# One streaming encoder layer on one core: root-scaled turning matmuls in the opening, and a last feed-forward group run by token halves

## The chip, the cores and the metric

The kernel runs on one core of one Trainium2 chip. The metric is device time in microseconds (us) for one launch, median over runs. Engines are named as in the profile: PE is TensorE (PEld its weight load), DVE is VectorE, ACT is ScalarE, POOL is GpSimd, SP is SyncE, which here issues DMAs. A bank is one of the eight 2-KB-per-partition buffers in which PE leaves its results.

## The reference, cut to what matters

One layer over 512 prompt tokens and 64 sample tokens (576 together), model width 1024, all in fp32:

```
n = rmsnorm(x, ln_mix);  proj = n @ w_in
h = x + W_out [ GDN(conv, gates of proj) ; DiffAttn(proj) ]
h = h + MemCrossAttn(rmsnorm(h, ln_mem_q))
h = h + W2 relu(W1 rmsnorm(h, ln_ffn))^2        (1024 -> 4096 -> 1024)
y = rmsnorm(h, ln_final)
rmsnorm(x, g) = x * rsqrt(mean(x*x) + 1e-6) * g
```

Outputs are y for both groups of tokens, and new caches and states. The change touches the first norm (and the turning of its result) and the last group of the feed-forward part with the final norm.

## The kernel before, in words

**Layout.** Activations are kept with features on partitions and tokens along the free axis, as `[128, 4, 576]` tiles, two for 1024 features. x arrives with tokens on partitions, as five token tiles (four of 128, one of 64; `TT`), and must be turned. Every projection is split for precision: an operand is held as `hi`, its value rounded to fp32r, and `lo`, the rest, and `project` (L150) adds hi x hi, hi x lo and lo x hi, so 24 matmuls for 1024 features into one bank. It does so for each of two token halves (`HALVES`: columns 0 to 256 and 256 to 576). `weights` (L141) loads 128 columns of a weight matrix into one of three `raw` tiles (tag `raw`, `bufs=3`), casts `hi` on ACT (L147) and subtracts `lo` on DVE (L148) into two buffers each (tags `wh`, `wl`).

**Who sets the order.** A scheduler orders each engine's queue by program order and readiness. The opening is written out by hand: inside `with in_order()` (L281) each engine's instructions keep the order of the program, though instructions from elsewhere may come between them.

**Opening (L204 to L331).** SP's queue loads, in this order, token tile 0, the row of `ln_mix` spread over 128 partitions (`gain_rows`, L117), tile 1, weights 4 of `w_in`, tiles 2 and 3, weights 5, tile 4, weights 6, and then the rows of all gains, of the convolution weights and of its state, into one tile `rows` of 126 partitions. For each token tile ACT squares and sums (`squares`, L190), DVE and POOL make the root (`root`, L195; `rpow` on POOL, L174), DVE scales the whole 128 x 1024 tile by root and gain (`scale`, L201), PE turns it in eight 128 x 128 transposes into two banks (`turn`, L204), ACT copies `hi` (L244) and DVE subtracts `lo` (L249). Between them PE runs the first token half of three projections (`first_half`, weights 4, 5, 6), as soon as tiles 0 and 1 are turned. The splits of weights 5 and 6 are on POOL (L304, L315). Last come the transpose of `rows` into the columns `gcol` and the third first half.

**Beside the opening.** PE also turns the unscaled x (8 x 5 transposes into banks `g0` and `g1`, L367) for the residual stream. It stands later in the program, but nothing holds it back: the scheduler puts these transposes wherever PE is free.

**End (L955 to L1000).** The feed-forward part is done in eight groups of 512 hidden features: `ff1(g)` makes four blocks of hidden features, `ff2(g)` adds their product to the residual `hT`, eight blocks of 128 output features, each for both token halves. ff1 of a group is issued ahead of ff2 of the group before. In the last group `add_residual(m, True)` also squares on ACT (L866, L869) and sums on DVE (L871). After it ACT multiplies each block by `ln_final` (L987), five matmuls against ones sum over the features for each token tile (`norm_columns`, L875), DVE and POOL make the roots, and for each token tile and half PE turns four blocks back into a bank of tag `ba` (which has two banks), ACT (half 0, L996) or DVE (half 1, L998) multiplies by the root, and SP stores the tile (L1000).

Banks by tag: `pr` 3, `ba` 2, `g0`, `g1` and `gs` one each.

## Time and profile before

| | us |
|---|---|
| runs shown, median of 3 | 1105.75 (1105.25 to 1108.7) |
| the profiled execution | 1104.43 |
| its span in the profile | 1102.7 |
| PE busy / idle in the span | 1056.7 / 46.0 |
| DVE, ACT, POOL busy | 623.8, 408.4, 78.6 |

In a row of the profile, `L98 PE MATMUL pr<-u,wh 128*128 128x256 f32 x16` is line 98, its engine and operation, the tile written and those read, the stationary and the moving shape, and the count. A row in order of time begins with its start and its length in us and ends with the idle time of the engine before it and what ended it. A row of groups has total busy time, mean in ns, and idle time before. An fp32 matmul appears as two instructions, an fp32r one and a transpose as one. A matmul's length contains the latency of the pipeline; the pace is read from a run of them.

### The profile page before, as it was taken

The page shows a single profiled execution, that of the slowest core. Times are in us where ns is not written, and L with a number is a line of the kernel's source. Part 1 is how long each engine was busy: PE and PEld are TensorE (multiplying, and loading weights), DVE is VectorE, ACT ScalarE, POOL GpSimd, SP SyncE. Part 2 cuts the span into 40 slices and gives each one's busy share as a digit, 9 for nine tenths or more (in the row PEclk, how much of TensorE's full clock was granted, in tenths as well). Part 3 has the DMA queues.
Part 4 walks back from the last instruction along what each step waited for, and adds up shares of the span by engine and source line. Part 5 has one row for each costly group of instructions (what it writes and reads, how often), then busy time and mean ns, then how long its engine had stood idle before and what let it go on. Part 6 is the DMA issues. An engine that isn't in the chain of part 4 may idle for free.

```text
span 1102.7 us, 18954 instructions
## 1 busy us (share of the span) xinstructions
PE 1056.7 (96%) x7708; PEld 1002.8 (91%) x7708; DVE 623.8 (57%) x1335; ACT 408.4 (37%) x842; POOL 78.6 (7%) x127
## 2 busy tenths in 40 slices
PE   5999899899999999899999999999999999999997
PEld 5999799888888888799988799999999999999996
DVE  6766674665455566355454555655555555455554
ACT  5533554233135557543332343322222222222244
POOL 5421120221000000000000000000000000000000
PEclk9999999999999999899999999999999999999998
DMA  7242310100122254434211032223323141414122
GB/s 220 84 141 71 117 39 21 41 20 12 48 78 60 91 171 118 134 117 151 69 47 39 23 93 78 59 72 92 86 77 96 58 116 49 115 50 114 58 78 86
DMA packets 151494, 90.62 MB, mean 82 GB/s; under 512 B 5472, under 2 KB 147934, under 8 KB 150896
## 3 DMA queue, kind: packets, MB, share of 16 engines
q1 hardware_dynamic: 151408, 89.41, 27.6%
q8 instruction: 61, 1.00, 0.4%
q14 instruction: 25, 0.20, 0.1%
HBM read 79.66 MB, written 9.74 MB: 81 GB/s over the span
## 4 chain that ended last, share of the span: by engine, by line
issue 41%; PE 30%; DVE 1%; DMA 1%; ACT 1%; POOL 1%; POOLq 0%; ACTq 0%; SPq 0%
PE pr L98 20%; PE g L98 4%; PE ba L102 3%; PE gs L98 2%; PE ba L98 2%; DMA out_dram<-p 1%; POOL ta L174 0%; DVE an L805 0%; POOL tiny L174 0%; PE g L102 0%; DVE u L998 0%; ACT p L840 0%; DVE wl L148 0%; POOLq L1031 0%; ACT p L927 0%
## 5 line engine op out<-in xcount | busy, mean ns | idle before, releaser
L98 PE MATMUL pr<-u,wh 128*128 128x256 f32 (+1 forms) x3936 | 811.5, 300 | 0.4
L98 PEld LDWEIGHTS pr<-u,wh 128*128 128x128 f32 x3936 | 638.2, 191 | 7.0 <-issue 2.0
L98 PE MATMUL pr<-u,wl 128*128 128x256 f32 (+1 forms) x1968 | 584.9, 298 | 0.0
L98 PEld LDWEIGHTS pr<-u,wl 128*128 128x128 f32 x1968 | 373.2, 190 | 1.3 <-issue 0.2
L147 ACT CAST wh<-raw 128x1024 fp32r<-128x1024 f32 (+1 forms) x161 | 141.4, 878 | 289.0 <-PE pr L98 266.2
L148 DVE TENSOR_TENSOR wl<-raw,wh 128x1024 fp32r<-128x1024 f32 (+1 forms) x161 | 163.0, 1012 | 66.5 <-ACT wh L147 62.2
L858 DVE TENSOR_TENSOR u<-u,pr 128x256 f32<-128x256 f32 (+1 forms) x160 | 72.4, 453 | 105.2 <-PE pr L98 105.2
L964 DVE TENSOR_TENSOR p<-pr,rB 128x256 f32<-128x256 f32 x64 | 29.3, 458 | 65.4 <-PE pr L98 65.4
L167 ACT CAST u<-p 128x256 fp32r<-128x256 f32 x64 | 27.8, 434 | 89.2 <-DVE p L965 87.5
L174 POOL TENSOR_TENSOR tiny<-tiny,nhalf 128x1 f32<-128x1 f32 (+2 forms) x10 | 10.3, 1032 | 658.7 <-DVE tiny L882 488.3
L168 DVE TENSOR_TENSOR u<-p,u 128x256 fp32r<-128x256 f32 x64 | 29.2, 457 | 20.2 <-ACT u L167 20.2
L98 PE MATMUL g<-u,qz 128*128 128x256 f32 (+4 forms) x96 | 29.2, 405 | 1.2 <-ACT p L781 1.2
L965 DVE SCALAR_TENSOR_TENSOR p<-p 128x256 f32<-128x256 f32 x64 | 29.3, 458 | 1.7
L102 PE MATMUL ba<-ident,u 128*128 128x128 f32 (+2 forms) x128 | 22.7, 318 | 6.0 <-ACT p L840 3.2
L355 DVE SCALAR_TENSOR_TENSOR p<-p,gcol,p 128x579 f32<-128x579 f32 x33 | 27.1, 820 | 0.9
L98 PE MATMUL g<-Dt,B 128*128 128x128 f32 (+1 forms) x200 | 26.6, 278 | 0.9 <-DVE B L571 0.9
L571 DVE SCALAR_TENSOR_TENSOR B<-lev,At 128x512 f32<-128x512 f32 (+1 forms) x30 | 20.9, 708 | 10.0 <-PE g L98 6.9
L98 PEld LDWEIGHTS g<-Dt,B 128*128 128x128 f32 (+1 forms) x200 | 22.7, 185 | 4.0 <-ACT X L602 2.9
L781 ACT ACTIVATE p<-g,ta 128x320 f32<-128x320 f32 (+4 forms) x40 | 21.2, 532 | 13.6 <-DVE ta L779 10.4
L98 PE MATMUL g<-Y,X 128*128 128x128 f32 (+1 forms) x192 | 25.6, 274 | 0.2
L602 ACT COPY X<-g 128x512 f32<-128x512 f32 (+1 forms) x24 | 13.2, 549 | 33.7 <-PE g L102 33.6
L170 ACT ACTIVATE u<-u,gcol 128x256 fp32r<-128x256 f32 (+1 forms) x32 | 17.1, 533 | 23.1 <-DVE u L858 23.1
(270 smaller groups left out, 981.6 us busy)
## 6 DMA issues: line engine op xcount, KB each, us to landing
raw<-in_w_ff_dram SPq DMA_DIRECT2D x32, 512.0 KB
raw<-in_w_ff_dram SPq DMA_DIRECT2D x64, 256.0 KB
raw<-in_w_in_dram SPq DMA_DIRECT2D x28, 512.0 KB
raw<-in_w_mem_k_dram SPq DMA_DIRECT2D x8, 512.0 KB
raw<-in_w_mem_v_dram SPq DMA_DIRECT2D x8, 512.0 KB
raw<-in_w_out_dram SPq DMA_DIRECT2D x8, 512.0 KB
raw<-in_w_mem_q_dram SPq DMA_DIRECT2D x8, 512.0 KB
raw<-in_w_mem_o_dram SPq DMA_DIRECT2D x8, 512.0 KB
```

The source lines that it names most:

```text
L98: nc.tensor.matmul(out, lhsT, rhs, start=start, stop=stop)
L102: nc.tensor.transpose(out, in_, ident[:n, :n])
L147: A.copy(wh, raw)
L148: V.tensor_tensor(wl, raw, wh.bitcast(F32), ALU.subtract)
L167: A.copy(h, src)
L168: V.tensor_tensor(lo, src, h.bitcast(F32), ALU.subtract)
L355: V.scalar_tensor_tensor(yv[:, :n], cb[:, i : i + n], cwt[:, m, i : i + 1], yv[:, :n], ALU.mult, ALU.add)
L571: V.scalar_tensor_tensor(B[:n, :, :n], lev[:n, :n].unsqueeze(1).to_broadcast([n, 4, n]), float(lv), At[:n, :, :n], ALU.is_equal, ALU.mult,)
L781: A.activation(p[:, :nk], b[:, :nk], AF.Exp, bias=mx[:, c : c + 1], scale=0.125, accum_out=l[:, c : c + 1])
L858: V.tensor_tensor(hm, hm, b, ALU.add)
L964: V.tensor_tensor(f, b, rB[:, a0 : a0 + n], ALU.mult)
L965: V.scalar_tensor_tensor(f, f, 0.0, f, ALU.max, ALU.mult)
```

## The change

Opening:

- The rows of the gains (42 partitions) are loaded first of all, on ACT's DMA queue, into a tile of their own; the rows of convolution weights and state stay last on SP's queue. The broadcast load of `ln_mix` is gone. PE turns the 42 rows into the columns `gmix` at once.
- x is not scaled. For each token tile DVE writes the roots on a diagonal (`root_diag`), and PE turns and scales in one matmul: stationary the 128 x 128 block of raw x, moving the diagonal (`turn_normed`). One bank now holds one block of 128 features for a whole token half.
- `hi_lo`: ACT makes `hi` with the gain as a column scale, DVE `lo` with a scalar_tensor_tensor. The first token half takes banks `pr` and `ba` in turn, the second `g0` and `ba`.
- The splits of weights 5 and 6 move from POOL to DVE.
- The order is: both first roots, split of weights 4, first half turned (root 2 after its fourth block), first halves with weights 4 and 5 with roots 3 and 4 in between, second half turned, convolution rows turned, first half with weights 6.
- The transposes of raw x and their copies are queued behind the last instruction of the opening on PE and on ACT. What followed POOL's last instruction of the opening follows DVE's last one instead, and so does the small lambda block.

End:

- While the second-last group's products run, the last group's weights are loaded, cast and split, all eight blocks, into tiles that ff1's input no longer needs.
- The last group runs its eight blocks for token half 0 and then for token half 1. The final gain is applied in the evacuation.
- Within the second pass PE also runs the root matmuls of token tiles 0 and 1 (after block 1), their turnings (after blocks 3 and 4) and the first-half turnings of tiles 2 to 4 (after block 6, into `g0`, `g1`, `gs`). Their first instructions are pinned to that place in PE's queue. After it come the roots of tiles 2 to 4 and the rest. Each token tile is stored in two halves.

The diff, cut to its core:

```diff
@@ -94,12 +95,16 @@
...
-    def mm(out, lhsT, rhs, start=True, stop=True):
-        nc.tensor.matmul(out, lhsT, rhs, start=start, stop=stop)
-    def tr(out, in_):
+    def mm(out, lhsT, rhs, start=True, stop=True, pin=False):
+        i = nc.tensor.matmul(out, lhsT, rhs, start=start, stop=stop)
+        if pin:
+            tc.keep_in_program_order(i)
+    def tr(out, in_, pin=False):
...
-        nc.tensor.transpose(out, in_, ident[:n, :n])
+        i = nc.tensor.transpose(out, in_, ident[:n, :n])
+        if pin:
+            tc.keep_in_program_order(i)
...
@@ -212,43 +216,50 @@
...
+    rows, crow = small("B0", [42, P]), small("B1", [84, P])
+    for i, g in enumerate((ln_mix[0], ln_mem_kv[0], ln_mem_q[0], ln_ffn[0], ln_final)):
+        nc.scalar.dma_start(rows[8 * i : 8 * i + 8, :], g.rearrange("(k p) -> k p", p=P))
+    nc.scalar.dma_start(rows[40:41, :], gdn_norm)
+    nc.scalar.dma_start(rows[41:42, :], diff_norm)
+    FIRST = (4, 5, 6)
+    raws = {}
...
-    gmix = gain_rows(ln_mix[0], "qz0")
...
-    FIRST = (4, 5, 6)
-    raws = {4: load(w2, 4 * P)}
+    raws[4] = load(w2, 4 * P)
...
-    rows = small("B0", [126, P])
-    for i, g in enumerate((ln_mix[0], ln_mem_kv[0], ln_mem_q[0], ln_ffn[0], ln_final)):
-        nc.sync.dma_start(rows[8 * i : 8 * i + 8, :], g.rearrange("(k p) -> k p", p=P))
-    nc.sync.dma_start(rows[40:41, :], gdn_norm)
-    nc.sync.dma_start(rows[41:42, :], diff_norm)
...
-        nc.sync.dma_start(rows[42 + 12 * i : 54 + 12 * i, :], conv_w[0, i].rearrange("(m p) -> m p", p=P))
+        nc.sync.dma_start(crow[12 * i : 12 * i + 12, :], conv_w[0, i].rearrange("(m p) -> m p", p=P))
...
-        nc.sync.dma_start(rows[90 + 12 * i : 102 + 12 * i, :], state_gdn_conv[0, 0, i].rearrange("(m p) -> m p", p=P))
-    tags = ("pr", "ba")
-    turned = {}
-    def turn_tile(t):
-        turned[t] = [turn(xn[t], TT[t][1], q, tags[q]) for q in range(2)]
-    def hi(t):
-        t0, n = TT[t]
-        for q in range(2):
-            A.copy(xh[q][:, :, t0 : t0 + n], turned[t][q])
-    def lo(t):
-        t0, n = TT[t]
-        for q in range(2):
-            V.tensor_tensor(
-                xl[q][:, :, t0 : t0 + n], turned[t][q], xh[q][:, :, t0 : t0 + n].bitcast(F32), ALU.subtract
-            )
+        nc.sync.dma_start(crow[48 + 12 * i : 60 + 12 * i, :], state_gdn_conv[0, 0, i].rearrange("(m p) -> m p", p=P))
+    diag = [small("aT", [P, 4, P]), small("aT", [P, 4, P])]
+    dg = [diag[t // 4][:, t % 4, :] for t in range(5)]
+    def turn_normed(k, half, tag):
+        a0, n = HALVES[half]
+        b = bank(tag)
+        for t in ((0, 1), (2, 3, 4))[half]:
+            t0, w = TT[t]
+            mm(b[:, t0 - a0 : t0 - a0 + w], xt[t][:w, k * P : (k + 1) * P], dg[t][:w, :w])
+        return b[:, :n]
+    def hi_lo(b, k, half):
+        a0, n = HALVES[half]
+        g = gmix[:, k : k + 1]
+        h, lo = (x[k // 4][:, k % 4, a0 : a0 + n] for x in xs)
+        A.activation(h, b, AF.Identity, scale=g)
+        V.scalar_tensor_tensor(lo, b, g, h.bitcast(F32), ALU.mult, ALU.subtract)
+    def root_diag(t, n):
+        s1 = tiny([P, 1])
+        A.activation(sqd[:n, :D], xt[t][:n], AF.Square, accum_out=s1[:n])
+        r1 = root(s1, n)
+        V.tensor_scalar(dg[t][:n, :n], ident[:n, :n], r1[:n], None, ALU.mult)
...
@@ -277,63 +288,47 @@
...
-    sqr, rts = {}, {}
-    with in_order():
-        sqr[0] = squares(xn[0], xt[0], P)
-        rts[0] = root(sqr[0], P)
-        scale(xn[0], xt[0], rts[0], gmix, P)
+    gps0 = bank("gs")
+    gmix = const([P, 42], "gmix")
+    with in_order() as opened:
+        tr(gps0[:, :42], rows)
+        V.tensor_copy(gmix, gps0[:, :42])
+        root_diag(0, P)
+        root_diag(1, P)
...
-        sqr[1] = squares(xn[1], xt[1], P)
-        rts[1] = root(sqr[1], P)
...
-        turn_tile(0)
-        hi(0)
-        sqr[2] = squares(xn[2], xt[2], P)
-        scale(xn[1], xt[1], rts[1], gmix, P)
-        turn_tile(1)
-        lo(0)
-        rts[2] = root(sqr[2], P)
-        hi(1)
-        lo(1)
+        for k in range(KT):
+            hi_lo(turn_normed(k, 0, ("pr", "ba")[k % 2]), k, 0)
+            if k == 3:
+                root_diag(2, P)
...
-        sqr[3] = squares(xn[3], xt[3], P)
-        rts[3] = root(sqr[3], P)
-        scale(xn[2], xt[2], rts[2], gmix, P)
-        turn_tile(2)
...
-        G.tensor_tensor(wts[5][1], raws[5], wts[5][0].bitcast(F32), ALU.subtract)
-        sqr[4] = squares(xn[4], xt[4], DEC)
-        rts[4] = root(sqr[4], DEC)
+        V.tensor_tensor(wts[5][1], raws[5], wts[5][0].bitcast(F32), ALU.subtract)
+        root_diag(3, P)
+        root_diag(4, DEC)
...
-        scale(xn[3], xt[3], rts[3], gmix, P)
-        scale(xn[4], xt[4], rts[4], gmix, DEC)
...
-        hi(2)
-        lo(2)
...
-        last_pool = G.tensor_tensor(wts[6][1], raws[6], wts[6][0].bitcast(F32), ALU.subtract)
-        turn_tile(3)
-        turn_tile(4)
-        hi(3)
-        lo(3)
-        hi(4)
-        lo(4)
+        V.tensor_tensor(wts[6][1], raws[6], wts[6][0].bitcast(F32), ALU.subtract)
+        for k in range(KT):
+            hi_lo(turn_normed(k, 1, ("g0", "ba")[k % 2]), k, 1)
...
-        tr(gps[:, :126], rows)
-        gcol = const([P, 126], "gcol")
-        V.tensor_copy(gcol, gps[:, :126])
+        tr(gps[:, :84], crow)
+        gcol = const([P, 84], "gcol")
+        last_dve = V.tensor_copy(gcol, gps[:, :84])
...
+    last_pool = zeroed[6]
...
-    gn = gcol[:, 40:41]
+    gn = gmix[:, 40:41]
...
-    V.tensor_scalar(dn, gcol[:, 41:42], 1.0 - LAM0, None, ALU.mult)
-    cwt = gcol[:, 42:].rearrange("p (s m) -> p m s", m=12)
+    V.tensor_scalar(dn, gmix[:, 41:42], 1.0 - LAM0, None, ALU.mult)
+    cwt = gcol.rearrange("p (s m) -> p m s", m=12)
...
@@ -363,8 +358,9 @@
...
-                for q in range(2):
-                    A.copy(hst[q][:, :, t0 : t0 + n], turn(xt[t], n, q, f"g{q}"))
+                with tc.issue_after(opened[mybir.EngineType.Activation]), tc.issue_after(opened[mybir.EngineType.PE]):
+                    for q in range(2):
+                        A.copy(hst[q][:, :, t0 : t0 + n], turn(xt[t], n, q, f"g{q}"))
...
@@ -463,7 +459,7 @@
...
-    with tc.issue_after(last_pool.ins):
+    with tc.issue_after(last_dve.ins):
...
@@ -968,36 +965,89 @@
...
-    def ff2(g, s):
-        for m in range(KT):
-            project(
-                weights(w_ff2[0, g * 512 : (g + 1) * 512, :], m * P, 4), s, add_residual(m, g == NG - 1), kt=4
-            )
+    wlast = []
+    def last_weights(m):
+        if m == 0:
+            wlast.extend(unit(i, [P, 4, 4, P], F32R) for i in (8, 7, 6, 4))
+        hi, lo = wlast[m // 4][:, m % 4], wlast[2 + m // 4][:, m % 4]
+        raw = wp.tile([P, 4, P], F32, tag="raw", name=nm("raw"), bufs=3)
+        nc.sync.dma_start(raw, w_ff2[0, (NG - 1) * 512 :, m * P : (m + 1) * P].rearrange("(k p) n -> p k n", p=P))
+        A.copy(hi, raw)
+        V.tensor_tensor(lo, raw, hi.bitcast(F32), ALU.subtract)
+    def last_block(m, s, a0, n):
+        hi, lo = wlast[m // 4][:, m % 4], wlast[2 + m // 4][:, m % 4]
+        def evac(b, a0, n):
+            add_residual(m, True)(b, a0, n)
+            hm = hT[m // 4][:, m % 4, a0 : a0 + n]
+            A.activation(hm, hm, AF.Identity, scale=gmix[:, G_FIN + m : G_FIN + m + 1])
+        project((hi, lo), s, evac, kt=4, halves=((a0, n),))
+    yo = {}
+    def turn_out(t, half, tag, pin=False):
+        t0, n = TT[t]
+        b = bank(tag)
+        for i in range(4):
+            tr(b[:n, i * P : (i + 1) * P], hT[half][:, i, t0 : t0 + n], pin=pin and i == 0)
+        return b
+    def put_out(t, half, b, r):
+        t0, n = TT[t]
+        if half == 0:
+            yo[t] = unit((10, 11, 2, 3, 5)[t], [P, 2, 512])
+            A.activation(yo[t][:n, half, :], b[:n], AF.Identity, scale=r[:n, t : t + 1])
+        else:
+            V.tensor_scalar(yo[t][:n, half, :], b[:n], r[:n, t : t + 1], None, ALU.mult)
+        dst = y_prompt[0, t0 : t0 + n] if t < 4 else y_sample[0]
+        nc.sync.dma_start(dst[:, 512 * half : 512 * half + 512], yo[t][:n, half, :])
+    def final_roots(ts, pin=False):
+        b = bank()
+        c = slice(ts[0], ts[-1] + 1)
+        r, r2 = tiny([P, 8]), tiny([P, 8])
+        V.memset(r, 1.0)
+        for t in ts:
+            t0, n = TT[t]
+            mm(b[:n, t : t + 1], accs[0][:, t0 : t0 + n], ones[:, 0:1], pin=pin and t == ts[0])
+            V.tensor_scalar(r[:n, t : t + 1], b[:n, t : t + 1], 1.0 / D, EPS, ALU.mult, ALU.add)
+        rpow(r2[:, c], r[:, c])
+        return r2
...
-        ff2(g - 1, pend)
+        for m in range(KT):
+            project(
+                weights(w_ff2[0, (g - 1) * 512 : g * 512, :], m * P, 4), pend, add_residual(m, False), kt=4
+            )
+            if g == NG - 1:
+                last_weights(m)
...
-    ff2(NG - 1, pend)
...
-        hm = hT[m // 4][:, m % 4, :]
-        A.activation(hm, hm, AF.Identity, scale=gcol[:, G_FIN + m : G_FIN + m + 1])
-    r = norm_columns()
-    for t, (t0, n) in enumerate(TT):
-        yo = unit((10, 11, 2, 3, 5)[t], [P, 2, 512])
-        for half in range(2):
-            b = bank()
-            for i in range(4):
-                tr(b[:n, i * P : (i + 1) * P], hT[half][:, i, t0 : t0 + n])
-            if half == 0:
-                A.activation(yo[:n, half, :], b[:n], AF.Identity, scale=r[:n, t : t + 1])
-            else:
-                V.tensor_scalar(yo[:n, half, :], b[:n], r[:n, t : t + 1], None, ALU.mult)
-        dst = y_prompt[0, t0 : t0 + n, :] if t < 4 else y_sample[0]
-        nc.sync.dma_start(dst, yo[:n].rearrange("p a b -> p (a b)"))
+        last_block(m, pend, *HALVES[0])
+    early = {}
+    for m in range(KT):
+        last_block(m, pend, *HALVES[1])
+        if m == 1:
+            r = final_roots((0, 1), pin=True)
+        if m in (3, 4):
+            t = m - 3
+            for half in range(2):
+                put_out(t, half, turn_out(t, half, "ba", pin=True), r)
+        if m == 6:
+            for t in (2, 3, 4):
+                early[t] = turn_out(t, 0, ("g0", "g1", "gs")[t - 2], pin=True)
+    r = final_roots((2, 3, 4))
+    for t in (2, 3, 4):
+        put_out(t, 0, early[t], r)
+        put_out(t, 1, turn_out(t, 1, "pr"), r)
...
```

Likewise left out are `lpr`, `le` and the lambda loads, which move unchanged under `tc.issue_after(last_dve.ins)`, the names `gcol` that become `gmix`, and `in_order`, which now yields the last instruction of each engine.

33 lines of the change are left out of this document (17 added, 16 removed).

## Prediction

> **What bounds the kernel now.** I read the page first (busy shares, slices, chain), then the busy time by stage (each row: the stretch, its length, busy time of PE, weight load, DVE, ACT and POOL with instructions, granted clock, DMA share, GB/s), then both ends of the kernel in order of time.
>
> ```profile
> span 1102.7 us, 18954 instructions
> PE 1056.7 (96%) x7708; PEld 1002.8 (91%) x7708; DVE 623.8 (57%) x1335; ACT 408.4 (37%) x842; POOL 78.6 (7%) x127
> PE   5999899899999999899999999999999999999997
> issue 41%; PE 30%; DVE 1%; DMA 1%; ACT 1%; POOL 1%; POOLq 0%; ACTq 0%; SPq 0%
> ...
> 0.00:10.00 10.00, 3.62 (x16) 3.25 (x17) 1.89 (x4) 4.86 (x9) 1.84 (x11) 1.00 0.84 264
> 10.00:20.00 10.00, 7.57 (x51) 7.33 (x49) 8.41 (x13) 7.32 (x14) 5.38 (x4) 0.83 0.73 186
> 20.00:30.00 10.00, 7.64 (x58) 7.20 (x56) 9.14 (x13) 4.92 (x10) 9.80 (x18) 0.89 0.68 168
> 60.00:70.00 10.00, 10.00 (x77) 10.00 (x76) 7.73 (x12) 2.79 (x6) 2.16 (x6) 1.00 0.54 148
> 1080.00:1090.00 10.00, 8.05 (x61) 7.51 (x60) 4.99 (x13) 4.79 (x9) 1.17 (x1) 0.96 0.01 2
> 1090.00:1103.00 13.00, 6.94 (x32) 5.15 (x32) 3.48 (x5) 3.17 (x5) 0.00 (x0) 0.63 0.49 182
> ```
>
> TensorE (PE) is busy for 96% and carries the chain ("issue" there is time in which it waited for nothing). The change touches its two thin ends: the first 30 us, where PE idles 6.38 + 2.43 + 2.36 = 11.2 us, and the last 23 us, where it idles 1.95 + 6.06 = 8.0 us. At 60 us it never idles, and by the slices hardly anywhere between, so work pushed from an end into the middle costs its full length.
>
> **The opening.** Rows in order of time, one of the stages, one of the chain, and the groups by shape:
>
> ```profile
> 4.46 1.06 ACT L192 ACTIVATE u<-u 128x1024 f32<-128x1024 f32 x1 [2.15 <-DMA u<-in_x_prompt_dram]
> 5.95 0.56 POOL L174 TENSOR_TENSOR tiny<-tiny,nhalf 128x1 f32<-128x1 f32 x1 [4.28 <-DVE tiny L197]
> 7.73 1.06 ACT L192 ACTIVATE u<-u 128x1024 f32<-128x1024 f32 x1 [2.12 <-DMA u<-in_x_prompt_dram]
> 9.64 0.69 DVE L285 CAST wh<-raw 128x1024 fp32r<-128x1024 f32 x1 [1.80 <-DMA raw<-in_w_in_dram]
> 10.36 1.23 DVE L288 TENSOR_TENSOR wl<-raw,wh 128x1024 fp32r<-128x1024 f32 x1
> 10.48 1.54 POOL L174 TENSOR_TENSOR tiny<-tiny,nhalf 128x1 f32<-128x1 f32 x1 [3.72 <-DVE tiny L197]
> 15.28 3.13 PE L98 MATMUL pr<-u,wh 128*128 128x256 f32 x16
> 19.20 0.60 PE L102 MATMUL pr<-ident,u 128*128 128x128 f32 x4
> 19.99 2.16 PE L98 MATMUL pr<-u,wh 128*128 128x256 f32 x16
> 22.13 3.42 DVE L202 SCALAR_TENSOR_TENSOR u<-u,tiny,gB 64x1024 f32<-64x1024 f32 x1 [0.44 <-POOL p L271]
> 27.74 4.60 PE L98 MATMUL pr<-u,u 128*128 128x256 f32 x24
> ...
> 27.70:30.00 2.30, 2.30 (x13) 2.30 (x12) 1.88 (x8) 1.23 (x3) 2.10 (x7) 0.50 0.33 33
> ...
> 273.59 0.60 PE g L98 x8
> ...
> L102 PE MATMUL g<-ident,u 128*128 128x128 f32 x20 | 4.6, 385 | 4.6 <-DMA u<-in_x_prompt_dram 4.6
> L170 ACT ACTIVATE u<-u,gcol 128x320 fp32r<-128x320 f32 x16 | 8.9, 559 | 0.0
> L170 ACT ACTIVATE u<-u,gcol 128x256 fp32r<-128x256 f32 x16 | 8.1, 508 | 23.1 <-DVE u L858 23.1
> L171 DVE SCALAR_TENSOR_TENSOR u<-u,gcol,u 128x320 fp32r<-128x320 f32 x16 | 8.7, 545 | 0.0
> L171 DVE SCALAR_TENSOR_TENSOR u<-u,gcol,u 128x256 fp32r<-128x256 f32 x16 | 7.7, 483 | 8.1 <-ACT u L170 8.1
> ```
>
> The mark is the end of the third first-half block (weights 6): 27.74 + 4.60 = 32.34 us, after which PE is full. A block is 24 matmuls: 0.12 us each at full clock (the row at 19.99, less the latency of its last), 0.2 at half clock (15.28: 3.13 us for 16; the granted clock of the 27.70 row is 0.50).
>
> The change, queue by queue:
> - **Second token tile.** The 512-KB broadcast of the gain between tiles 0 and 1 goes. The two took 7.73 - 4.46 = 3.27 us, so tile 1 lands near 4.46 + 1.63 = 6.1 (bounds 6.1 and 7.73), and weights 4 by about 8.0. The seven row loads move from SP's queue to ACT's, ahead of its first squares; ACT has little else until 4.46, so I cost them at nothing (if that cover fails, +1). DVE's queue now begins with the copy of these rows, and everything on DVE waits if they land after 7.
> - **Roots.** POOL starts 0.43 after the squares end (5.95 against 5.52) and takes 0.56, since DVE stands still for it (1.54, beside the 1.23-us DVE operation, is the other bound); the diagonal is an eighth of the 0.69-us cast's width, say 0.25 (bounds 0.1 and 0.69). 6.1 + 1.06 + 0.43 + 0.56 + 0.25: both diagonals stand at 8.4. The full-width scalings, the 3.42 at 22.13 among them, vanish.
> - **First turning.** DVE casts and splits weights 4 (0.69 + 1.23) up to 10.4 and then subtracts eight times 0.48. Between the fourth and fifth it stands for tile 2's root: ACT has done four 0.51-us copies by 11.2, then 1.06 + 0.43 + 0.56 + 0.25 make 13.5. Last subtraction at 15.5. PE turns for the same price as before: an fp32 128x128 matmul is two instructions, four of them take 0.60 us (273.59), as do four transposes (19.20). The first block ends at 16.6 at full clock, 17.7 at half.
> - **Second block:** 24 x 0.12 = 2.9, so 19.5, or up to 21.4. DVE's splits of weights 5 and 6, taken over from POOL (1.23 each), and the roots 3 and 4 lie under it.
> - **Second turning.** Every other one goes to g0, which has one bank: matmuls 0.4, ACT 0.56, DVE 0.55, handovers 0.25 make 1.76 us for two, so eight take some 6.2: 25.7 to 27.6. Queued behind them on PE are the transpose of the convolution rows and block three.
> - **Third block,** 2.9 or 4.6: it ends between 28.6 and 32.2. I take 30.0, a mix of clocks, since PE works about half of the second turning. That is 2.3 us earlier.
> - **The moved transposes.** The 20 of the x20 row lie in the opening's gaps. They are now queued behind the opening, where PE never idles: 20 x 0.15 = **3.0 us later** there. Their ACT copies hide (ACT works 2.79 of 10 us at 60).
>
> Opening: +3.0 - 2.3 = **+0.7 us**, bounds -0.7 (28.6) and +2.9 (32.2).
>
> The Trainium skill, "TensorE: Matmul & The Clock Gate", section Terms, says that transpose mode is 4 times faster for fp32, which speaks against plain matmuls here. By it the sum would be larger by 40 x 3 x 0.15 = 18 us of PE time, an estimate; the rows at 273.59 and 19.20 disagree, and the measurement decides.
>
> **The end.** Rows in order of time, the stores by tile, and stages:
>
> ```profile
> 1085.47 0.31 PE L98 MATMUL pr<-u,wl 128*128 128x320 f32 x1
> 1087.38 0.81 PE L98 MATMUL ba<-ones,p 128*128 128x1 f32 x6 [0.77 <-DVE p L871]
> 1089.73 0.69 ACT L996 ACTIVATE u<-ba,tiny 128x512 f32<-128x512 f32 x1 [2.12 <-POOL tiny L174]
> 1097.79 0.74 DVE L998 TENSOR_SCALAR u<-ba,tiny 64x512 f32<-64x512 f32 x1 [0.72 <-PE ba L102]
> L1000 SPq DMA_DIRECT2D out_dram<-u x5: 332/356/472, 1090.6 to 1098.6; - x5
> ...
> 1098.00:1099.00 1.00, 0.00 (x0) 0.00 (x0) 0.54 (x1) 0.00 (x0) 0.00 (x0) 1.00 0.99 406
> 1100.00:1101.00 1.00, 0.00 (x0) 0.00 (x0) 0.00 (x0) 0.00 (x0) 0.00 (x0) 0.50 0.90 193
> 1101.00:1102.00 1.00, 0.00 (x0) 0.00 (x0) 0.00 (x0) 0.00 (x0) 0.00 (x0) 0.50 0.01 0
> ...
> 1060.07 0.62 ACT L147 CAST wh<-raw 128x512 fp32r<-128x512 f32 x1 [2.58 <-PE pr L98]
> 1060.72 0.69 DVE L148 TENSOR_TENSOR wl<-raw,wh 128x512 fp32r<-128x512 f32 x1
> 1063.00:1063.50 0.50, 0.50 (x6) 0.50 (x5) 0.08 (x1) 0.19 (x1) 0.00 (x0) 1.00 1.01 302
> 1063.50:1064.00 0.50, 0.50 (x6) 0.50 (x6) 0.44 (x2) 0.49 (x2) 0.00 (x0) 1.00 0.01 3
> ```
>
> The last product ends at 1085.78; the roots are out 3.95 us later (1089.73), ten evacuations end at 1098.53, data stops moving just before 1101, and the span ends about 2 us after that.
>
> The products of the last group stay the same in number. PE gains, ahead of the last one, 28 transposes (0.15 each: 4.2) and four root matmuls (6 in 0.81: 0.55): last product at 1085.78 + 4.75 = 1090.5. The first half's norm is complete more than a block before PE reaches its matmuls, and each output turning has its bank back a block later. The root chain stays 3.95: 1094.5. Then three ACT evacuations (0.69) run beside three on DVE (0.74): done at 1096.8, 1.7 us sooner. Now the stores are late: 1.25 MB fall due in 2 us instead of 8. The first is issued (0.36) at 1095.2 and moves an estimated 0.9 later; 1 MB at the 406 GB/s seen takes 2.6 us, the 64-row tile's 256 KB at 193 GB/s 1.35, so data ends at 1100.0 and the span 2 us behind, at 1102.0: -0.7. One wait is new. The roots are columns of one bank, and now DVE reads each column before the program's next root matmul writes its neighbour (before, all five matmuls came first). If PE must wait for that read, with all the products queued behind it, it costs two handovers and a short DVE operation, about 0.4: once in the second pass, twice at the end, 1.2 in all. No row shows it; between 0 and 1.2 I take 0.9, since both touch one tile. End: **+0.2 us**, bounds -2.5 (no such wait, transposes hidden in part, all stores at 406 GB/s) and +1.5 (a stall at a pinned turning besides).
>
> Moved into group 6: eight more weight loads, casts (0.62) and splits (0.69). ACT then casts for 1.24 and DVE splits for 1.38 of each block of 3.2 us (12 matmuls of 0.12, 12 of 320 columns at 0.15); they hide as long as the three raw tiles suffice.
>
> **Sum.** +0.7 + 0.2 = +0.9 us on the profiled execution's 1104.43 (span 1102.7 and 1.7 around it), 1105.3. The median of the runs shown is 1105.75; I predict **1106.6**.
>
> **The rivals.**
> - *Slower: the raw tiles run out.* In group 6 two loads per block pass through three tiles; each holds one for the issue, the landing, the cast and the split (1.31), and every other one waits for a weight buffer besides. Walked through block by block, PE stalls nowhere up to a landing 3.0 us after the issue, and 3.7 us in all at 4. For: nothing else here loads at this rate. Against: the load freed by the split's end at 1061.41 had stopped moving by 1063.5, so it lands after some 2.1 to 3. At 4 us: 1106.6 + 3.7 = 1110.3.
> - *Slower: half clock all through the opening.* Third block at 32.2: +2.9 + 0.2, 1108.9, just within 0.3%.
> - *Slower: turning matmuls at four times the 0.15.* 9.6 and 14 us of PE in turnings that last 7 and 6.2: +10, 1116.6. Against: the row at 273.59 is the same form.
> - *Faster: the moved transposes find idle PE after all,* -2.3 + 0.2: 1103.7; or both ends reach their good bounds, -0.7 - 2.5: 1102.5; both together, 1099.5. Against: they are early in the program, and the middle is full.
> - *A little faster: full clock from the first block,* since turnings are now plain matmuls: 28.6, so -0.7 + 0.2, 1105.2. The slow row at 15.28 came right after transposes. The Trainium skill's same page, section "Part 4: PE-mode transpose", says that transposes do not count as activity for the clock; the row agrees.
>
> **How the numbers follow.** A measurement of this kernel can tell about 0.3%, 3.3 us. Forecast, both ends near even: 0.36; full clock 0.10; half clock 0.10; raw tiles, or another stall that the newly ordered queues make in the middle, 0.20; dear matmuls 0.03; idle transposes or good bounds 0.21, of which 0.18 passes 3.3 us. Faster 0.18; slower 0.23 and 0.04 of the half clock, 0.27; the rest, 0.55, same. Range 1101.5 to 1111: it takes in the rivals but the dear matmuls, longer landings and the two good cases together.
>
> **What would show it.** Right: turnings start near 8.4, the third block ends near 30, all 40 raw transposes lie behind it, the span ends 11 to 12 us after the last product instead of 16.9. Wrong: PE idle in group 6 with a DMA behind it; turnings at over 0.2 us a matmul; rows landing after 7; PE waits in the middle that are not there now.

## The result and the profile after

After takes **1112.09 us** (median of 4 runs, 1111.75 to 1112.48), before in the same comparison 1105.5 (1104.23 to 1108.7): a ratio of 1.0055, 95% interval [1.0034, 1.0077]. The forecast was 1106.6 in 1101.5 to 1111, so the change is slower by 6.6 us and the time lies above the range. The profiled execution of after took 1111.75 us, its span 1110.0. Unless a ratio to another kernel is named, every ratio below is to before in the same comparison. One run of all was slow, 1162.09 us at a granted clock of 0.85, and it is the only one of its kernel (the second of experiment 6) with a trace.

The page of after (span, busy shares), then the busy time by stage in the columns that the prediction explains:

```profile
span 1110.0 us, 19049 instructions
PE 1061.5 (96%) x7749; PEld 1006.9 (91%) x7749; DVE 620.9 (56%) x1348; ACT 411.1 (37%) x854; POOL 68.2 (6%) x126
...
10.00:20.00 10.00, 9.80 (x59) 9.16 (x60) 7.16 (x15) 7.12 (x14) 1.29 (x3) 1.00 0.81 188
20.00:30.00 10.00, 9.40 (x65) 7.94 (x63) 4.83 (x10) 4.89 (x11) 2.70 (x8) 1.00 0.56 130
50.00:60.00 10.00, 7.80 (x52) 7.50 (x50) 7.33 (x10) 6.08 (x13) 1.82 (x7) 0.83 0.19 54
```

From 10 to 30 us PE is busier than before, and the clock column reads 1.00 where before had 0.83 and 0.89. That looks like the gain that was wanted, but the busy time is dearer work, and up to 15 us the pace is that of half clock all the same (rows at 14.03 and 15.39 below). And there is a new hole at 50 to 60 us: PE works 7.80 of 10 us there and the clock falls to 0.83; before, PE was full from 30 to 110 us.

To see where the time goes, I follow marks that both kernels have. The last copy of a convolution state (the last of the POOL group below, on L358 before and L353 after) stands at the end of the convolution stage. The group's columns are minimum, median and maximum duration in ns, then the first and the last start in us.

```profile
L358 POOL COPY cst<-p x11: 185/971/1272, 37.1 to 104.4; 128x3 f32<-128x3 f32 x11
```

```profile
L353 POOL COPY cst<-p x11: 187/979/981, 40.1 to 112.9; 128x3 f32<-128x3 f32 x11
```

| mark | before | after | later by |
|---|---|---|---|
| third first-half block ends | 32.34 | 34.55 | 2.2 |
| last convolution-state copy | 104.4 | 112.9 | 8.5 |
| last evacuation of the first feed-forward product starts | 1034.6 | 1044.1 | 9.5 |
| last product ends | 1085.78 | 1098.69 | 12.9 |
| span ends | 1102.7 | 1110.0 | 7.3 |

So the first 113 us lose 8.5, the middle 1.0, and the end wins 2.2. The loss of 8.5 falls into parts that can be seen. First the opening, in order of time:

```profile
8.01 0.30 PE L105 MATMUL gs<-ident,B 42*128 42x42 f32 x1 [8.01 <-DMA B<-in_diff_norm_dram]
8.35 0.20 DVE L295 COPY gmix<-gs 128x42 f32<-128x42 f32 x1 [7.41 <-PE gs L105]
10.54 0.29 DVE L262 TENSOR_SCALAR aT<-ident,tiny 128x128 f32<-128x128 f32 x1 [0.71 <-POOL tiny L178]
14.03 1.06 PE L99 MATMUL pr<-aT,u 128*128 128x128 f32 x4
15.39 0.61 PE L99 MATMUL pr<-aT,u 128*128 128x128 f32 x4
15.84 0.61 PE L99 MATMUL ba<-aT,u 128*128 128x128 f32 x4
22.61 0.97 PE L99 MATMUL g<-aT,u 128*128 128x128 f32 x6
24.79 1.07 PE L99 MATMUL g<-aT,u 128*128 128x128 f32 x6 [0.20 <-DVE u L256]
27.07 1.07 PE L99 MATMUL g<-aT,u 128*128 128x128 f32 x6 [0.20 <-DVE u L256]
31.44 3.11 PE L99 MATMUL pr<-u,u 128*128 128x256 f32 x24
```

The gain rows land at 8.0, the copy at the head of DVE's queue runs at 8.35, and the second diagonal at 10.54 to 10.83 instead of 8.4. In the first turning a block of two matmuls took 0.86 us up to the one that starts at 14.89 (14.89 - 14.03), and 15.84 - 15.39 = 0.45 after it: half pace and full pace, though the clock column reads 1.00 for both. In the second turning a pair of blocks takes 27.07 - 24.79 = 2.28 us where 1.76 was forecast.

Then the hole. These are PE, ACT and two stages of after:

```profile
51.35 1.03 PE L105 MATMUL g<-ident,u 128*128 128x128 f32 x8
55.65 1.72 PE L105 MATMUL g<-ident,u 128*128 128x128 f32 x8 [2.19 <-ACT u L363]
...
53.12 0.63 ACT L351 ACTIVATE u<-p 128x512 f32<-128x512 f32 x1 [2.22 <-DVE p L350]
53.66 1.03 ACT L151 CAST wh<-raw 128x1024 fp32r<-128x1024 f32 x1
55.01 1.07 ACT L363 COPY u<-g 128x512 f32<-128x512 f32 x2
...
55.65:58.00 2.35, 2.35 (x12) 2.33 (x13) 2.17 (x5) 1.60 (x3) 0.54 (x2) 0.57 0.33 81
58.00:60.00 2.00, 2.00 (x14) 1.93 (x12) 1.25 (x2) 1.05 (x2) 0.23 (x2) 0.66 0.55 167
```

The transposes of the unscaled x (PE L105) have one buffer of each of two banks. The first eight run at 51.35. The next eight need the banks back, and the copies that free them (ACT L363) stand in ACT's queue behind a Silu (L351), which waits 2.22 us for DVE's convolution, and behind a weight cast. PE waits 2.19 us with all the products queued behind the transposes. Right after it the granted clock is at a half: (1 - 0.57) x 2 x 2.35 + (1 - 0.66) x 2 x 2.00 = 3.4 us of half clock. Before's profile has no PE wait at all between 30 and 60 us.

At the end of after:

```profile
1095.46 1.03 PE L105 MATMUL g<-ident,u 128*128 128x128 f32 x8
1096.33 0.60 PE L105 MATMUL gs<-ident,u 128*64 128x128 f32 x4
1096.69 2.00 PE L99 MATMUL pr<-u,u 128*128 128x320 f32 x12
1103.06 1.27 ACT L1003 ACTIVATE u<-g,tiny 128x512 f32<-128x512 f32 x2 [2.75 <-POOL tiny L178]
```

Eight transposes between two products take 1096.33 - 1095.46 = 0.87 us, 0.11 each. From the last feed-forward evacuation to the last product's end it is 54.6 us instead of 51.2 (+3.4), and from there to the span's end 11.3 instead of 16.9 (-5.6).

### The profile page after: what moved, and what is told of

The parts are those of the page before. It is cut to its first block, busy times and chain, and to the rows that moved or that the text cites. A ratio compares the mean times of both kernels' runs of the same rounds, so it can differ in the third digit from the quotient of the medians.

```text
span 1110.0 us, 19049 instructions
## 1 busy us (share of the span) xinstructions
PE 1061.5 (96%) x7749; PEld 1006.9 (91%) x7749; DVE 620.9 (56%) x1348; ACT 411.1 (37%) x854; POOL 68.2 (6%) x126
## 4 chain that ended last, share of the span: by engine, by line
PE 58%; issue 2%; DVE 1%; ACT 0%; POOL 0%; DMA 0%; POOLq 0%; DVEq 0%; ACTq 0%
PE pr L99 52%; PE ba L99 2%; PE g L99 2%; PE ba L105 2%; PE gs L99 0%; DMA out_dram<-p 0%; POOL tiny L178 0%; DVE p L926 0%; DVE an L802 0%; POOL ta L178 0%; DVE u L1005 0%; ACT p L924 0%; ACT p L837 0%; ACT u L808 0%; POOLq L1081 0%
## 5 line engine op out<-in xcount | busy, mean ns | idle before, releaser
L99 PE MATMUL pr<-u,wh 128*128 128x320 f32 (+1 forms) x3808 | 787.3, 300 | 0.4
L99 PEld LDWEIGHTS pr<-u,wh 128*128 128x128 f32 x3808 | 617.8, 191 | 7.4 <-issue 2.0
L99 PE MATMUL pr<-u,wl 128*128 128x320 f32 (+1 forms) x1904 | 566.5, 299 | 0.0
L99 PEld LDWEIGHTS pr<-u,wl 128*128 128x128 f32 x1904 | 361.5, 190 | 1.3 <-issue 0.2
L151 ACT CAST wh<-raw 128x1024 fp32r<-128x1024 f32 (+1 forms) x153 | 136.9, 895 | 274.2 <-PE pr L99 253.8
L152 DVE TENSOR_TENSOR wl<-raw,wh 128x1024 fp32r<-128x1024 f32 (+1 forms) x153 | 157.5, 1030 | 70.3 <-ACT wh L151 67.1
L178 POOL TENSOR_TENSOR tiny<-tiny,nhalf 128x1 f32<-128x1 f32 (+4 forms) x11 | 8.0, 725 | 664.0 <-DVE tiny L1013 551.2
L99 PE MATMUL pr<-u,u 128*128 128x256 f32 (+1 forms) x240 | 33.7, 298 | 0.0
L99 PEld LDWEIGHTS pr<-u,u 128*128 128x128 f32 x240 | 32.2, 190 | 0.0
L778 ACT ACTIVATE p<-g,ta 128x320 f32<-128x320 f32 (+4 forms) x40 | 21.2, 533 | 12.8 <-DVE ta L776 10.4
L174 ACT ACTIVATE u<-u,gmix 128x256 fp32r<-128x256 f32 (+1 forms) x32 | 17.1, 534 | 23.2 <-DVE u L855 23.2
```

Source lines behind the costliest of these rows:

```text
L99: i = nc.tensor.matmul(out, lhsT, rhs, start=start, stop=stop)
L151: A.copy(wh, raw)
L152: V.tensor_tensor(wl, raw, wh.bitcast(F32), ALU.subtract)
L778: A.activation(p[:, :nk], b[:, :nk], AF.Exp, bias=mx[:, c : c + 1], scale=0.125, accum_out=l[:, c : c + 1])
```

## Experiments

**Theory A:** the loss is made in the opening and by the held-back transposes; the end wins 2.2. Rivals: the end loses too (B); the opening's own lateness is all of it (C); the copies' wait only moves (D).

**1. The end alone, and the opening alone.** The first kernel is before with the new end (the last hunk of the diff, with `gcol` for `gmix`), the second is after with the old end.

> The opening of before with the new end (last feed-forward group by halves, roots and output of the first half under the second). Theory A (the loss is made in the opening and the first 60 us, the end gains): no loss up to the last product, +3.4 us of added PE work there, 5.6 us less from the last product to the span's end, so 2.2 us less than before, about 1103.3. Rival B (the end loses as well, because the new stage's transposes and roots on TensorE cost more than the shorter tail gives): 1105.5 to 1108.

Measured: 1103.9 us, 0.998 [0.997, 0.9989]. A holds for the end.

The trace of this kernel shows one thing more. PE's instructions come in the same order as in before up to the last group, but in this execution the third block ended at 26.16 + 3.11 = 29.27, 3.1 us earlier than in before's profile. Two rows of it, then one of before:

```profile
51.55 0.66 PE L104 MATMUL g<-ident,u 128*128 128x128 f32 x4 [2.32 <-ACT u L371]
50.92 0.86 ACT L371 COPY u<-g 128x512 f32<-128x512 f32 x2
```

```profile
50.99 0.86 ACT L367 COPY u<-g 128x512 f32<-128x512 f32 x2
```

The copies of the unscaled x run at the same time in both, so PE, being early, waits 2.32 us for them, and the last convolution-state copy comes at 104.2 against 104.4. The wait for these copies is therefore not the new opening's alone, and an earlier third block is not worth its full length as long as they stand where they do in ACT's queue.

> The new opening with the end of before. Theory A: the whole loss and the end's missing gain, 8.5 to 9.5 us over before, 1114 to 1115. Rival B (the opening's lateness is made good in the middle, and the end loses): 1106 to 1110.

Measured: 1112.41 us, 1.0063 [1.005, 1.0075]. The opening makes the whole loss, though less than A said, and between the bounds of the two theories. Against before's 1105.66 in this comparison the two parts are +6.8 and -1.8, which add up to 5.0 us and not to the 6.6 of both; the intervals are wide enough for that. The old end was 1 us shorter here (67.1 us from the last feed-forward evacuation's start to the span's end, against 68.1 in before), since its half-clock stretch was over sooner.

**2. The held-back transposes, freed or put first.**

```diff
-                with tc.issue_after(opened[mybir.EngineType.Activation]), tc.issue_after(opened[mybir.EngineType.PE]):
-                    for q in range(2):
-                        A.copy(hst[q][:, :, t0 : t0 + n], turn(xt[t], n, q, f"g{q}"))
+                for q in range(2):
+                    A.copy(hst[q][:, :, t0 : t0 + n], turn(xt[t], n, q, f"g{q}"))
```

> After, with the forty turnings of the unscaled x for the residual no longer held behind the opening on TensorE and ScalarE: the planner may put them where it likes, as before. Theory A (3.0 us of moved transposes, 2.2 us of a wait for ScalarE's copy and about 1 us of half clock behind it all come from holding them back): 4 to 6 us less than after, about 1107. Rival C (the opening's own steps are late, and turnings among them delay the subtractions further): 1111 to 1114.

Measured: 1107.99 us, 1.0019 [1.0009, 1.0029]. The scheduler (the planner of the expectations) put 20 of the 40 transposes back into the opening's gaps; the third block still ended at 34.6, so they cost nothing there. In the second kernel they stay behind the opening, with `tc.high_priority()` added to the two holds.

> After, with the forty turnings of the unscaled x still behind the opening, but ahead of the convolution's work in ScalarE's queue, between the first projection's matmuls. Theory A (the wait of 2.2 us and the half clock come from ScalarE's copies queued behind Silu, which waits for VectorE): these 3 us go and the 3.0 us of moved transposes stay, about 1109. Rival D (the wait only moves, since ScalarE has sixteen copies of 0.5 us to do there and the first convolution then starts later): 1112 to 1114.

Measured: 1107.96 us, 1.002 [1.001, 1.0029], a little better than A's 1109. The convolution-state copies of the two kernels:

```profile
L353 POOL COPY cst<-p x11: 185/968/974, 40.2 to 109.1; 128x3 f32<-128x3 f32 x11
...
PE g L105 <- ACT u L362: 2.1, 1, 2.1
```

```profile
L353 POOL COPY cst<-p x11: 190/974/1002, 44.5 to 109.2; 128x3 f32<-128x3 f32 x11
```

The first kept the wait of 2.1 us (the row is a wait: engine and tile, releaser, us in total, times, longest) but not the half clock behind it; the second lost both. Each has the stage's end 3.7 to 3.8 us earlier than after. D and C fall. How much the place behind the opening costs can be read here too: from the end of the third block to the last state copy it is 109.2 - 34.55 = 74.6 us in the second kernel, which has neither the wait nor the half clock, and 104.4 - 32.34 = 72.1 in before, so 2.6 us.

**3. The gain copy behind the diagonals.**

```diff
-        V.tensor_copy(gmix, gps0[:, :42])
         root_diag(0, P)
         root_diag(1, P)
+        V.tensor_copy(gmix, gps0[:, :42])
```

> After, with the copy of the turned gain rows placed behind both diagonals in VectorE's written order, so that the diagonals no longer stand behind the rows' landing. Theory A (the rows land late and the copy at the head of the queue holds the diagonals back to 10.8 us): diagonals at about 8.5, first turning, its projection and everything behind 2.0 to 2.3 us earlier (third first-half block ends at 32.3 instead of 34.6), about 1110. Rival (the loads of tiles 2 to 4 or the cold clock set the pace anyway): third block at 34 to 34.6, 1112.

Measured: 1111.74 us, 1.0045 [1.0031, 1.0059], and the third block ended at 34.72. Theory A fails here: the copy was not all that held the second diagonal. In order of time, POOL and DVE of this kernel:

```profile
7.33 0.71 POOL L470 TENSOR_SCALAR_AFFINE_SELECT X<-X 128x128 f32<-128x128 f32 x1
9.89 0.56 POOL L178 TENSOR_TENSOR tiny<-tiny,nhalf 128x1 f32<-128x1 f32 x1
...
6.92 0.29 DVE L262 TENSOR_SCALAR aT<-ident,tiny 128x128 f32<-128x128 f32 x1 [0.75 <-POOL tiny L178]
10.49 0.28 DVE L262 TENSOR_SCALAR aT<-ident,tiny 128x128 f32<-128x128 f32 x1 [3.02 <-POOL tiny L178]
```

The first diagonal came 2.4 us sooner, at 6.92. The second root stood on POOL behind the building of the level masks (the L470 row is one of its steps), which the scheduler had put between the two roots as soon as there was room. A wait in DVE's queue had become one in POOL's.

The run tells something else for nothing. It has the wait at 50 to 60 us (2.2), but no half clock behind it (1.00 throughout), and its last state copy is at 111.7 instead of 112.9 while its third block is 0.2 later: that stretch of half clock costs about 1.4 us, by one profile of each kernel.

**4. The price of a turning matmul.** The diagonal holds ones instead of roots, so the scaling is left out, and the turning is a transpose with the same waits.

```diff
-            mm(b[:, t0 - a0 : t0 - a0 + w], xt[t][:w, k * P : (k + 1) * P], dg[t][:w, :w])
+            nc.tensor.transpose(b[:, t0 - a0 : t0 - a0 + w], xt[t][:w, k * P : (k + 1) * P], dg[t][:w, :w])
...
-        V.tensor_scalar(dg[t][:n, :n], ident[:n, :n], r1[:n], None, ALU.mult)
+        V.tensor_scalar(dg[t][:n, :n], ident[:n, :n], r1[:n], 0.0, ALU.mult, ALU.is_gt)
```

> After, with the turning matmuls replaced by transposes of the same tiles with the same waits (the diagonals hold ones where the root is positive, so x is turned unscaled and the projection's input lacks the root). Theory A (the step that failed is the price of a turning matmul, forecast like a transpose at 0.15 us): second turning 6.2 to 7 us instead of 8.75, first turning about 1 us shorter, third block at 31 to 32, 1109. Rival (VectorE's and ScalarE's splits and their banks set the pace of the turning): second turning 8 us or more, 1111 to 1112.

Measured: 1106.29 us, 1.0004 [0.9993, 1.0015], 5.8 us less than after, more than A said.

```profile
22.83 0.64 PE L248 MATMUL g<-aT,u 128*128 128x128 f32 x3 [0.63 <-DVE u L256]
23.40 0.64 PE L248 MATMUL ba<-aT,u 128*128 128x128 f32 x3
24.67 0.64 PE L248 MATMUL g<-aT,u 128*128 128x128 f32 x3 [0.63 <-DVE u L256]
28.47 4.76 PE L99 MATMUL pr<-u,u 128*128 128x256 f32 x24
...
26.00:28.00 2.00, 1.64 (x6) 0.75 (x5) 1.01 (x2) 0.99 (x2) 0.00 (x0) 0.50 0.09 22
```

At full clock a block of three takes 23.40 - 22.83 = 0.57 us and a pair 24.67 - 22.83 = 1.84, near the 1.76 of the forecast: the model of the ring of banks was right and its price wrong. As plain matmuls a block takes 1.00. But with transposes the clock fell to 0.50 and the third block took 4.76 us instead of 3.11. It still ended 1.3 us earlier, at 33.23. The convolution stage ended 4.5 earlier (108.4): the other 3.2 are the wait for ACT's copies, which shrank from 2.2 to 0.4 us, and the 1.4 of half clock, which did not follow. So the cheaper price bought only 1.3 us in the opening itself, net of the clock that it lost.

**5. A fourth bank in the second turning.**

```diff
-            hi_lo(turn_normed(k, 1, ("g0", "ba")[k % 2]), k, 1)
+            hi_lo(turn_normed(k, 1, ("g0", "ba", "g1", "ba")[k % 4]), k, 1)
```

> After, with the second turning rotating over four banks instead of three (the even blocks alternate between two buffers instead of one). Theory A2 (a block of three matmuls, its rounding and its subtraction hold the one bank in a ring of 2.27 us a pair): 1.0 to 2.5 us less in the second turning, third block at 32 to 33.6, about 1110. Rival (TensorE's own price of 0.97 us a block sets it): 8 blocks of 0.97 are 7.8, 1 us less at most, 1111 to 1112.

Measured: 1110.34 us, 1.0032 [1.0021, 1.0043].

```profile
22.36 0.97 PE L99 MATMUL g<-aT,u 128*128 128x128 f32 x6
30.29 0.29 PE L105 MATMUL gs<-ident,B 84*128 84x84 f32 x1
```

Eight blocks now take 30.29 - 22.36 = 7.9 us instead of 8.7: no wait for a subtraction is left, and the rival's price, 1.00 us a block, is the bound. Of the 2.5 us by which the second turning overran the forecast, the ring was worth 0.8 and the price the rest. The third block's end (33.48) and the time lie where A2 put them, the turning where the rival did; the median fell by 1.8 us against after's, and 1.1 of it is seen in the stage (last state copy at 111.8).

**6. Mending the opening.** One kernel takes edits 3 and 5, turns the unscaled tiles 0 and 1 at written places in the opening, and puts the other three behind it as in the second kernel of experiment 2:

```diff
         root_diag(0, P)
         root_diag(1, P)
         V.tensor_copy(gmix, gps0[:, :42])
+        keep_raw(0)
...
+        keep_raw(1)
         b4 = first_half(4)
```

> After, with four edits that answer the theory: gain copy behind the diagonals, four banks in the second turning, the unscaled tiles 0 and 1 turned in the opening at written places (before the first turning and between it and the first projection block), the other three behind the opening but first in ScalarE's queue. If the account of the loss holds (2.2 us opening, 3.0 moved transposes, 2.2 wait, 1 half clock; end 2 us gained), 2.4 of the 3.0, the wait, the half clock and 2 to 4 of the opening come back: 1101 to 1104. If the terms hide one another: 1105 to 1108.

Measured: 1102.53 us, 0.9963 [0.995, 0.9977], with no PE wait between 10 and 62 us. From the third block's end to the last state copy it is 106.0 - 33.41 = 72.6 us instead of after's 78.3, so 5.8 us came back, against 2.4 + 2.2 + 1.4 = 6.0 by the terms (transposes, wait, half clock): there they add. The stage ends 6.9 us earlier than in after; the other 2.7 of the 9.6 us by which the median is lower lie behind it and are not explained by the edits. The stage still ends 1.6 us later than before's.

Then theory A3, that the second root has to pass the mask work too. With edit 3 alone:

```diff
-    with tc.issue_after(last_dve.ins):
+    with tc.issue_after(last_dve.ins), tc.issue_after(pows[1].ins):
         lev = const([P, P], "lev")
```

> The kernel with the gain copy behind the diagonals, and GpSimd's building of the level masks held until the second tile's root is through it. Theory A3 (once the gain rows no longer hold VectorE, the second root stands behind the mask work that the planner had put on GpSimd from 6.8 to 9.9 us, and the diagonal still came at 10.5): second diagonal at about 8.5, third first-half block at 32 to 32.6 instead of 34.6, 1109 to 1110. Rival (something else, such as the cold clock at 0.85 us a block, then keeps the turning late): diagonal early, but third block at 33.5 or later, 1111 to 1112.

Measured: 1109.15 us, 1.0023 [1.0015, 1.0032], 2.6 us less than with edit 3 alone. A3 holds: in its trace the second diagonal stands at 8.00 + 0.34 = 8.34, and the third block ends at 32.85, at a granted clock of 0.85 from 20 us on. With it in the four-edit kernel, where the rows' transpose also moves behind `keep_raw(0)`:

> The kernel with the four edits, with the mask work held behind the second root too and the gain rows turned behind tile 0's unscaled turning on TensorE. Theory A3: first turning starts at 8.7 to 9 instead of 10.0, third block 1 to 2 us earlier, 1100.5 to 1101.5. Rival (the cold clock eats it): 1102 to 1103, no change from the four edits.

Measured: 1103.26 us, 0.9964 [0.9952, 0.9977]: no gain over the four edits.

```profile
8.05 0.34 DVE L264 TENSOR_SCALAR aT<-ident,tiny 128x128 f32<-128x128 f32 x1 [0.68 <-POOL tiny L178]
...
27.96 3.12 PE L99 MATMUL pr<-u,u 128*128 128x256 f32 x24
...
L365 POOL COPY cst<-p x11: 189/972/995, 39.0 to 103.6; 128x3 f32<-128x3 f32 x11
```

The second diagonal stands at 8.39, the forecast's 8.4, and the third block starts 2.3 us earlier than with the four edits (27.96 against 30.30); the stage ends 2.4 us earlier (103.6 against 106.0). Yet the profiled spans are 1099.9 and 1099.4. From the memset of the gate vector `gg` (at about 120 us) to the last feed-forward evacuation the one takes 914.9 us and the other 911.9, and the clock differs (granted clock is the third number from the end):

```profile
120.00:200.00 80.00, 74.54 (x584) 69.32 (x581) 50.34 (x103) 39.01 (x63) 13.41 (x12) 0.98 0.17 52
200.00:300.00 100.00, 93.80 (x752) 84.43 (x752) 59.07 (x135) 29.11 (x55) 17.70 (x15) 0.98 0.12 32
```

```profile
120.00:200.00 80.00, 74.23 (x590) 68.64 (x589) 50.52 (x108) 40.85 (x66) 12.61 (x12) 1.00 0.19 56
200.00:300.00 100.00, 92.98 (x760) 83.48 (x758) 59.75 (x138) 29.08 (x55) 18.53 (x16) 1.00 0.11 32
```

The four-edit kernel, the second fence, had no half clock in these two stages; the other had some in both, 3.4 us each. From 440 to 460 us it is the other way round (0.74 in the four-edit kernel, 0.83 in the other), so the whole stretch has 10.2 us of half clock against 13.6, which is worth 1.7 of the 3.0 us. The rest stays open, and all of it rests on two profiled executions.

**7. What the end gains from.** Before's opening and the last group by halves, but everything of the output after the last product:

```diff
-        if m == 1:
-            r = final_roots((0, 1), pin=True)
-        if m in (3, 4):
-            t = m - 3
-            for half in range(2):
-                put_out(t, half, turn_out(t, half, "ba", pin=True), r)
...
+    r = final_roots((0, 1))
+    for t in (0, 1):
+        for half in range(2):
+            put_out(t, half, turn_out(t, half, "ba"), r)
```

> The opening of before and the last group by halves, but roots, turnings and stores of the first half's tiles after the last product, as for the second half. If the end's gain comes from the output under the second half: last product 2.2 us (16 transposes and two root matmuls) earlier, but the tail is about as long as before or longer, 1106 to 1109, slower than before. If it comes from the halves' order alone: 1103 to 1104.

Measured: 1103.48 us, 0.9973 [0.9962, 0.9984]. No gain is seen from the output under the second half, the point of this part of the change: the whole new end has 0.998 [0.997, 0.9989]. What is left is either the halves or the banks that the turnings go to. Before, with one line changed:

```diff
-            b = bank()
+            b = bank(("ba", "pr", "g0", "g1", "gs")[(2 * t + half) % 5])
```

> The kernel before with one edit at its end: the ten output turnings cycle over five kinds of bank instead of sharing one kind with two buffers. Theory E (outputs placed under the second half brought nothing, since leaving them at the end cost nothing; what the new end gains is that the turnings no longer wait for two banks at half clock): the tail shrinks by about 2 us, 1103 to 1104, as with the whole new end. Rival (the last group's order by halves brings the gain, since the norm's last step is then 320 columns of one block behind the last product): 1105 to 1106, as before.

Measured: 1102.31 us, 0.9959 [0.9945, 0.9972]. One line does at least as well as the whole new end, with the old order of the blocks, so more banks are enough for the gain; the order by halves without them was not run. A stage of before's tail, then the tail of this kernel:

```profile
1090.00:1092.00 2.00, 1.53 (x7) 1.53 (x8) 0.48 (x1) 0.80 (x2) 0.00 (x0) 0.50 0.31 125
```

```profile
1087.81 0.31 PE L98 MATMUL pr<-u,wl 128*128 128x320 f32 x1
1092.13 0.69 ACT L996 ACTIVATE u<-ba,tiny 128x512 f32<-128x512 f32 x1 [2.17 <-POOL tiny L174]
1095.02 0.74 DVE L998 TENSOR_SCALAR u<-gs,tiny 64x512 f32<-64x512 f32 x1
...
1090.00:1092.00 2.00, 2.00 (x20) 1.97 (x19) 0.22 (x2) 0.00 (x0) 1.07 (x1) 1.00 0.00 0
1094.00:1096.00 2.00, 0.98 (x9) 0.71 (x7) 1.64 (x3) 1.24 (x2) 0.00 (x0) 1.00 1.01 406
```

Before, two banks made each turning wait for an evacuation, PE stood while the root was made, and the turnings then ran at half clock: ten evacuations ended 1098.53 - 1085.78 = 12.8 us after the last product. With five kinds of bank most turnings are done while the root is on its way, the clock stays at 1.00, and the evacuations end 1095.76 - 1088.12 = 7.6 us after it. The stores then come in one burst at 406 GB/s, and the tail is 13.8 us instead of 16.9.

**8. Mended opening with that end.** The four-edit kernel, and the one with the masks held as well, each with the old end and its changed line:

> The opening with the four edits, and the end of before with its turnings cycling over five kinds of bank (as in the run before). If the mended opening is worth the 1 to 2 us that the four-edit kernel was ahead of the new end alone: 1100.5 to 1101.5. If opening and end hide one another, or the opening is no better than the one of before: 1102 to 1103.

> The same with the mask work behind the second root and the gain rows behind the first unscaled turning. If time won in the opening reaches the end one for one: 2 us less than the run beside it, 1098.5 to 1100. If the half-clock stretches of the middle take it back, as the two like kernels with the new end suggest: within 1 us of the run beside it.

Measured: 1101.64 us, 0.9955 [0.994, 0.997], and 1100.4 us, 0.9948 [0.9929, 0.9966]. The second is the fastest here, about 6 us below before and 11.7 below after. The first lies between its two forecasts, and so does the second, 1.2 us below the first. Beside the one-line kernel (0.9959 [0.9945, 0.9972]) the medians are 0.7 and 1.9 us lower, and the intervals overlap. The last state copy comes at 105.9 and 103.7, in the one-line kernel at 104.9: the stage of the opening is longer in the first of the two and 1.2 us shorter in the second. So the four edits alone are not shown to beat before's opening, and whether the second does stays open.

## Why the prediction was wrong, point by point

- **Second token tile:** right, squares on it start at 6.11.
- **Rows of the gains "at nothing":** they landed at 8.0, the case "if they land after 7" that the text named with "everything on DVE waits". But its price was not DVE's alone. Freed of the rows, the second root stood behind mask work on POOL, a queue that the forecast did not look into; freed of both, the diagonal came at 8.39.
- **"PE turns for the same price as before":** the step that failed in the opening. The row at 273.59 that was quoted for a 128x128 matmul names no shape, and the eight instructions in it are 64x64. In order of time, before had both shapes (the first row is three matmuls, 0.28 us each with the latency of the last):

```profile
269.84 0.83 PE L98 MATMUL g<-Y,X 128*128 128x128 f32 x6
273.52 0.68 PE L98 MATMUL g<-Dt,At 64*64 64x64 f32 x8
```

  At full clock two turning matmuls take 15.84 - 15.39 = 0.45 us, 0.22 each and not 0.15, and a block of three 1.00 instead of some 0.45. Second turning: 8.7 us instead of 6.2. The rival of four times the price was too dear, and the factor of 4 that the prediction weighed (the Trainium skill, "TensorE: Matmul & The Clock Gate", section Terms) did not show either: 1.00 against 0.57 a block is 1.8.
- **First and second block, clock:** the pace was that of full clock from 14.9 on and stayed so, the third block took 3.11 us; the mix that was assumed was too slow. Against the full-clock bound of 28.6 the block ended 6.0 late, 3.0 of it by the last subtraction of the first turning (18.5 instead of 15.5; 2.4 of that is the late diagonal) and 2.5 in the second turning.
- **Moved transposes, 3.0 us:** mis-sized a little, and the transposes' pace elsewhere was 0.11 and not 0.15. With 20 of them back in the opening and no half clock the stage ended 3.8 earlier; less the 1.4 for the clock that is 2.4 (2.6 by the second kernel of experiment 2).
- **"Their ACT copies hide (ACT works 2.79 of 10 us at 60)":** the step that cost most, and failed. The share at 60 us is not the queue at 52 us, where the copies stand behind a Silu that waits for DVE. Cost: 2.2 us of PE wait and 1.4 of half clock. The prediction had this only as an unspecific stall in the middle.
- **The third block's end as the mark:** the forecast counted each us there as a us at the end (-2.3). The end-alone kernel reached the mark 3.1 us before before's profile and had 0.2 of it left at the last state copy, since PE then waited for the same copies. So even the forecast opening would probably have won less than was put down, as long as the copies stay where they are.
- The sum of the first 113 us: 2.2 (third block) + 2.4 + 2.2 + 1.4 = 8.2 of the 8.5 measured, forecast +0.7. It is a sum against the one profile of before.
- **End, +0.2:** it gave -2.2. The transposes cost 0.11 each between products and not 0.15 (28 x 0.11 and 0.3 for the roots are the 3.4 measured, not 4.75), and the tail was 11.3 us. The order PE, DVE, PE for the root columns is there, but roots came 1103.06 - 1098.69 = 4.4 after the last product, 0.4 and not 0.9 beyond 3.95. The sign was wrong by the sizes; and the mechanism "output under the second half" was not seen to pay, as experiment 7 shows.
- **Rivals:** the raw tiles did not run out, PE is without a wait in the last group. The half clock through the opening did not come; full clock did, from 14.9 us on.
- **The signs:** of the four signs of being wrong that the text named, three came: rows after 7 (8.0), turning matmuls at over 0.2 us (0.22), and a PE wait in the middle (2.2).

## What to carry to other kernels

A price taken from a row must have the row's shape beside it. A step that is pushed behind others waits in the queues of every engine that it touches, so look at the order in those queues at the place where it lands, and at what their heads wait for; a busy share does not tell it. Where a tail turns and evacuates through two banks, try more banks before moving work. Time won at an early mark counts only as far as no later step waits for something that the gain does not move.

## What the hardware showed beside

- The half clock comes in pieces. The granted clock in the traces is 0.50 for 3.4, 6.8 or 10.2 us at a time, at a few places of the program, and not every execution has them at all of these places: over the middle, 17.0 us of half clock in the end-alone kernel and 13.6 in before, whose instructions come in the same order up to the last group, and that stage takes 916.3 us in the one and 914.6 in the other. The Trainium skill, "TensorE: Matmul & The Clock Gate", section "What's actually happening", says that activity is judged in free-running windows of 3.4 us; these pieces agree. So differences of 1 to 3 us between two profiles of this kernel need a look at the clock first.
- With transposes in the second turning the clock fell (0.50 at 26 us in experiment 4), with plain matmuls in the same place it stayed at 1.00, so the block behind it took 3.11 us there against 4.76. PE also stood 0.63 us a pair in the one and 0.20 in the other; whether it was the kind of instruction or the idle time was not separated.
